# A hybrid decoder layer on one core: weight sums made ahead for ten groups instead of eight, and their casts one step later

## The chip, the cores and the metric

The kernel runs on one core of a Trainium2 chip. A core has five engines that work side by side, each through its own instructions in order: TensorE (PE, matrix products; PEld is its weight load), VectorE (DVE), ScalarE (ACT), GpSimd (POOL) and SyncE (SP, which here issues nearly all transfers). They wait for each other through semaphores. The metric is the time of one execution in microseconds on the device; lower is better.

## What is computed

One decoder layer for 256 tokens of width 2048, all in float32:

```python
h = layer_norm(alpha * h + 0.5 * swiglu(h, w_ffn1_gu, w_ffn1_down))
rq, rk, rv, rg, aq, ak, av, gate_r, gate_a = split(h @ w_in)
ret_branch = (silu(rg) * head_group_norm(retention(rotary(rq), rotary(rk), rv))) @ w_ret_out
att_branch = sliding_window_attention_sinks(rotary(aq), rotary(ak), av) @ w_att_out
mixed = (sigmoid(gate_r) * ret_branch + sigmoid(gate_a) * att_branch) @ w_mix_out
h = layer_norm(alpha * h + mixed)
h = layer_norm(alpha * h + 0.5 * swiglu(h, w_ffn2_gu, w_ffn2_down))
h = layer_norm(alpha * h + sigmoid(h @ w_ple_gate) * (p @ w_ple_proj))
```

The feed-forwards have an inner width of 5632, the retention 8 heads, the attention 16 query heads and 4 key heads with a window of 128.

## The kernel before

**Products of split numbers.** TensorE gets each float32 operand as two parts: a high part, which is the number rounded to the type fp32r (a cast on ScalarE, L98), and a low part, the number less its high part (a subtraction on VectorE, L99). A product is the sum of three: low by high, high by high, high by low (`Sum.add`, L374 to L376). So every 512 KB chunk of weights (128 x 1024 numbers) costs one load on SP, one cast and one subtraction before TensorE can use it. In the features form (`features_chunk`, L325 and L333) the weights are the stationary side.

**Seven products instead of eight.** Two halves of the tokens, two of the inner dimension and two of the outer make a 2 x 2 block product. A unit of kind "P" is one plain pair of chunks: 2 x 12 = 24 matmuls of 512 columns. A unit of kind "S" (`Seven`) gets by with seven products, 21 matmuls, and needs four sums of weights t1 to t4 (VectorE, 128 x 512 each), which are split like weights. A unit of kind "D" (`Prepared`) is the same, but its sums were made and split much earlier and put away in DRAM; the unit loads the four tiles hu, lu, hv, lv (high and low part of u = t1, t3 and of v = t2, t4), one chunk and half of another.

**The second feed-forward** (`ffn("f2", ...)`) has eleven blocks j of columns, each of eight pairs p of the inner dimension. `gu_units` names the kinds: block 0 is plain; blocks with even j have four S; blocks with odd j have three S, or three S and two D (pairs 4 and 5, `AHEAD`) if j stands in `AHEAD_BLOCKS`. The order in a D block is "PPSDSDSP", in the other odd ones "PPSPSPSP". After each block its 128 x 512 result is transposed on TensorE (L906), two chunks into the next block.

**Sums made ahead** (`sums_ahead`) is a generator: each step is one call of `next` from `run_side`, which runs after each chunk or unit of weights, first the next job of the list `side`, then one step of the first generator in the list `lazy`. For each item it makes u (L238, L239), casts it (L240), makes v (L242, L243), casts it (L244), loads the next item's two raw chunks, subtracts (L248 for u, L250 for v) and stores the four tiles (L252, L255); `pause` waits `every` steps between these. Items are listed block by block, pair 4 then pair 5. Items 0 and 1 run during queries and keys of the retention, items 2 to 4 during its values, item 5 during its gates, items 6 and 7 in the last projection of the mixers (`w_mix`).

**Around it.** `fill` loads and splits weights ahead of use as far as a budget of slots and of time allows; `slots_for_weights` sets the budget. All tiles of up to 512 KB share 46 slots. Before unit 0 of a D block the budget is set to `AHEAD_SLOTS - j`. The retention gates (`paired_out(("w_in_f2", grp), ...)`, tiles rg) run with the retention's own work in `side`, two heads at a time: `ret2` (outputs ro on TensorE, L1187, then statistics on VectorE, L1194), `ret2b` (the reciprocal root, ten small instructions, and the normalization, L1206), `ret2c` (times the gate, L1216), `ret3` (four transposes on TensorE, L1225), `ret3b` (L1236, L1237). Each job stands one chunk after the one before; a chunk of gates is twelve matmuls.

The order of the work is written out by hand; nothing is reordered.

Of the kernel before, what the change touches and what calls it, by code (L numbers as in the profile page):

```python
# [39 lines left out]


AHEAD = (4, 5)
AHEAD_BLOCKS = (1, 3, 5, 7)
AHEAD_SLOTS = 32

SEVEN_DOWN = (6, 7, 8, 9)
# [9 lines left out]
def layer(ctx: ExitStack, tc: tile.TileContext, io):  # L56
# [16 lines left out]
    def slot(shape, dt, name):  # L73
        return slots.tile(shape, dt, tag="slot", name=name)
# [144 lines left out]
    def sums_ahead(items, wait, every):  # L219


        def pause():
            for _ in range(every):
                yield

        pairs = [[Chunk(k) for k in items[0]]]
        for _ in range(wait):
            yield
        for j, (key, _) in enumerate(items):
            a, b = pairs.pop()  # L230
            b11, b21, b12, b22 = a.of(a.raw, 0), a.of(a.raw, 1), b.of(b.raw, 0), b.of(b.raw, 1)
            u, v = (slot([P, 2, 512], F32, w + a.name) for w in "uv")
            t1, t3, t2, t4 = (x.rearrange("p (g n) -> p g n", g=2) for x in (u[:, 0], u[:, 1], v[:, 0], v[:, 1]))
            parts = [slot([P, 2, 512], F32R, w + a.name) for w in ("hu", "lu", "hv", "lv")]
            uh, ul, vh, vl = parts
            away = [dram.tile([P, 2, 512], F32, name=f"{w}{a.name}") for w in ("hud", "lud", "hvd", "lvd")]
            put_by_sums[key] = away
            dve.tensor_tensor(t1, b11, b12, ALU.add)  # L238
            dve.tensor_tensor(t3, b12, b22, ALU.add)  # L239
            act.copy(uh, u)  # L240
            yield from pause()
            dve.tensor_tensor(t2, b11, t3, ALU.add)  # L242
            dve.tensor_tensor(t4, t2, b21, ALU.add)  # L243
            act.copy(vh, v)  # L244
            if j + 1 < len(items):
                pairs.append([Chunk(k) for k in items[j + 1]])
            yield from pause()
            dve.tensor_tensor(ul, u, uh, ALU.subtract)  # L248
            yield from pause()
            dve.tensor_tensor(vl, v, vh, ALU.subtract)  # L250
            for e in range(2):
                sync.dma_start(away[e], parts[e].bitcast(F32))  # L252
            yield from pause()
            for e in range(2, 4):
                sync.dma_start(away[e], parts[e].bitcast(F32))  # L255
# [44 lines left out]
    def slots_for_weights(n, ahead=45, far=90):  # L300
        room.update(slots=n, ahead=ahead, far=far)
# [5 lines left out]
    lazy = []  # L307
# [152 lines left out]
    def forms_of(parts, name):  # L460
        hi, lo = (slot([P, 8, P], F32R, name + w) for w in "hl")
        return seven_forms(whole(parts, name + "w"), hi, lo)

    def units_of(order, sevens, ahead=()):

        sevens, ahead = list(sevens), list(ahead)
        plain = [p for p in range(KD // 2) if p not in sevens + ahead]
        of = {"S": sevens, "D": ahead, "P": plain}
        return [(kind, of[kind].pop(0)) for kind in order]
# [382 lines left out]
    def gu_units(name, j):  # L852
        if j == 0:
            return [("P", p) for p in range(KD // 2)]
        if name == "f2" and j in AHEAD_BLOCKS:
            return units_of("PPSDSDSP", SEVEN[:3], AHEAD)
# [3 lines left out]
    def gu_keys(name, j):  # L860
        return lambda n, p: (name + "_gu", j, n, p)
# [26 lines left out]
    def ffn(name, i, ht, norm, keep, residual, keepers, away):  # L888
# [28 lines left out]
        for j in range(KF // 4):  # L917
# [19 lines left out]
            def before(u, j=j, offset=KD // 2 - len(units)):  # L937
# [7 lines left out]
                if j == 0 and u == 7:  # L945
# [3 lines left out]
                    if name == "f2":  # L949
                        g = AHEAD[0] // 2  # L950
                        made[g] = forms_of([ht[:, 4 * g : 4 * g + 4, :]], f"{name}f{g}")
                if name == "f2" and j in AHEAD_BLOCKS and u == 0:
                    slots_for_weights(AHEAD_SLOTS - j)
# [151 lines left out]
    def mixers(ht, norm, residual, keepers, away):  # L1105
# [29 lines left out]
        slots_for_weights(14)  # L1135
        ahead = [(gu_keys("f2", j)(0, p), gu_keys("f2", j)(1, p)) for j in AHEAD_BLOCKS for p in AHEAD]
        lazy.append(sums_ahead(ahead[:2], 3, 2))
        lazy.append(rotary_table("a"))
        lazy.append(sums_ahead(ahead[2:5], 2, 2))
        lazy.append(sums_ahead(ahead[5:6], 3, 4))  # L1140
        for grp in range(8):
            ps = banks(f"rqk{grp}")
            features_out([(("w_in_f", grp), ps)], KD, both_halves)
# [310 lines left out]

        lhs = lambda k: of_pairs(mix_t, k)
        slots_for_weights(16)
        lazy.append(sums_ahead(ahead[6:], 3, 2))
        for blk in range(3):
            if blk == 2:
                load_for_norm(1)  # L1460
# [195 lines left out]
    with tc.manual_schedule():  # L1656
        dve.memset(warm, 0.0)
        for eps, v in roots.items():
            dve.memset(v, 4.0 * eps)
        act.activation(warm, warm, AF.Silu)  # L1660
        plan_ffn("f1")
        plan.extend(Single(("w_pp", blk, 0)) for blk in range(2))
        plan_mixers()
        plan.extend(Single(("w_pp", blk, 0)) for blk in range(2, 4))
        plan_ffn("f2")
        for blk in range(4):
            plan_tokens(("w_pg", blk), KD)
        kept = sorted({p // 2 for p in SEVEN})
        warm_up()
        norm = ffn("f1", 0, ht, None, x_parts, x_columns, (), rows[0])  # L1670
        norm = mixers(norm.new, norm, rows[0], kept, rows[1])
        norm = ffn("f2", 2, norm.new, norm, norm.keep, rows[1], (), None)
        embedding(norm.new, norm, norm.y)
        assert not (plan or loaded or ready or side or lazy) and not room["used"]
# [100 lines left out]
```

## Time and profile before

| | us |
|---|---|
| median of three runs (lowest, highest) | 2276.21 (2275.74, 2276.75) |
| the profiled execution's own time | 2275.9 |
| its span in the profile | 2274.1 |
| TensorE busy | 2262.9 |
| VectorE busy | 1980.2 |
| ScalarE busy | 1219.8 |

The profile is one execution, in which each instruction has a start and a length. Views of it sum instructions by line, tile and operation, list them in order of time, sum them over stretches of the span, or follow the chain of work that ended last back from its end. A tile's name ends in what it holds: hw_in_f is the high part of a chunk of w_in, lw_in_f the low part, rw_in_f the raw chunk. "x4" counts instructions in one row; a figure in brackets is idle time of the engine before the instruction, with what ended it. A matmul's length includes its way through the array: the next one starts before it ends, so distances are taken from start to start. On VectorE too an instruction can start a little before the one ahead of it ends.

### The profile page before, as it was taken

The numbers are of one execution on the slowest core, as the hardware profiler recorded it, in microseconds if no ns is written. First come the engines' busy times: TensorE is split into PE (matmuls) and PEld (weight loads), VectorE is DVE, ScalarE is ACT, GpSimd is POOL, SyncE is SP. The second block draws the span as 40 slices with busy tenths as digits, with TensorE's granted clock in tenths as the row PEclk, the third lists the DMA queues.
The fourth block names the chain that finished last, engine by engine and source line by source line (L and its number), as shares of the span: only waits on it lengthen the run. The fifth ranks groups of instructions, "written<-read, shape, count | busy, mean of one in ns | idle before, by whom it ended". The sixth has DMA issues, their size and how long they took to land.

```text
span 2274.1 us, 29070 instructions
## 1 busy us (share of the span) xinstructions
PE 2262.9 (100%) x10495; PEld 1880.3 (83%) x10495; DVE 1980.2 (87%) x2561; ACT 1219.8 (54%) x1485; POOL 2.2 (0%) x9
## 2 busy tenths in 40 slices
PE   9999999999999999999999999999999999999998
PEld 8888888888888888888778888888888888888886
DVE  7999999999989887787789787789999999889887
ACT  6555555556555444544566454555565556555543
POOL 0000000000000000000000000000000000000000
PEclk9999999999999999999999999999999999999999
DMA  8666665665587789655456567787767766565772
GB/s 300 204 203 196 196 212 177 206 205 190 206 290 255 259 307 310 222 163 169 141 158 221 187 211 268 293 287 237 263 213 260 253 197 216 193 213 189 284 268 75
DMA packets 207592, 505.75 MB, mean 222 GB/s; under 512 B 16076, under 2 KB 19788, under 8 KB 207448
## 3 DMA queue, kind: packets, MB, share of 16 engines
q1 hardware_dynamic: 205320, 501.06, 65.5%
q10 hardware_dynamic: 2128, 2.84, 0.4%
q8 instruction: 82, 1.34, 0.2%
q14 instruction: 62, 0.51, 0.1%
HBM read 478.67 MB, written 25.17 MB: 222 GB/s over the span
## 4 chain that ended last, share of the span: by engine, by line
PE 97%; DVE 1%; DMA 1%; issue 0%; ACT 0%; POOL 0%; DVEq 0%; ACTq 0%; POOLq 0%
PE f1g L376 3%; PE f1g L374 3%; PE f1g L375 3%; PE f2g L376 3%; PE f2g L375 3%; PE f2g L374 3%; PE rqk L325 3%; PE f1u L376 2%; PE f1u L375 2%; PE f1u L374 2%; PE f2u L376 2%; PE f2u L375 2%; PE f2u L374 2%; PE aqk L325 2%; PE f2d L375 2%; PE f1d L375 2%
## 5 line engine op out<-in xcount | busy, mean ns | idle before, releaser
L99 DVE TENSOR_TENSOR lf_gu<-rf_gu,hf_gu 128x1024 fp32r<-128x1024 f32 (+1 forms) x276 | 325.3, 1210 | 14.1 <-ACT hf_gu L98 13.2
L98 ACT CAST hf_gu<-rf_gu 128x1024 fp32r<-128x1024 f32 (+1 forms) x276 | 275.7, 1043 | 31.7 <-DMA rf_gu<-in_f_gu 30.0
L99 DVE TENSOR_TENSOR lf_down<-rf_down,hf_down 128x1024 fp32r<-128x1024 f32 x152 | 181.2, 1219 | 23.6 <-ACT hf_down L98 20.3
L99 DVE TENSOR_TENSOR lw_in_f<-rw_in_f,hw_in_f 128x1024 fp32r<-128x1024 f32 x140 | 167.2, 1218 | 34.5 <-ACT hw_in_f L98 34.5
L98 ACT CAST hf_down<-rf_down 128x1024 fp32r<-128x1024 f32 x152 | 155.6, 1051 | 77.5 <-DMA rf_down<-in_f_down 21.5
L98 ACT CAST huf_gu<-uf_gu 128x1024 fp32r<-128x1024 f32 x70 | 73.7, 1053 | 145.4 <-DVE uf_gu L171 139.7
L98 ACT CAST hw_in_f<-rw_in_f 128x1024 fp32r<-128x1024 f32 x140 | 139.9, 1050 | 1.9 <-PE ga0a L375 1.0
L374 PE MATMUL f1g<-hf_gu,xt 128*128 128x512 f32 x247 | 96.6, 391 | 0.0
L376 PE MATMUL f1g<-lf_gu,xt 128*128 128x512 f32 x247 | 96.4, 390 | 0.0
L375 PE MATMUL f1g<-hf_gu,xt 128*128 128x512 f32 x247 | 96.4, 390 | 0.0
L98 ACT CAST hvf_gu<-vf_gu 128x1024 fp32r<-128x1024 f32 x70 | 73.8, 1054 | 29.5 <-DVE vf_gu L173 28.5
L963 ACT ACTIVATE eve<-eve 128x1024 f32<-128x1024 f32 x20 | 21.2, 1062 | 125.8 <-DVE eve L962 125.8
L374 PE MATMUL f2g<-hf_gu,ht 128*128 128x512 f32 x223 | 87.0, 390 | 0.0
L376 PE MATMUL f2g<-lf_gu,ht 128*128 128x512 f32 x223 | 86.9, 390 | 0.0
L375 PE MATMUL f2g<-hf_gu,ht 128*128 128x512 f32 x223 | 86.8, 389 | 0.0
L99 DVE TENSOR_TENSOR luf_gu<-uf_gu,huf_gu 128x1024 fp32r<-128x1024 f32 x70 | 85.2, 1217 | 0.0
L99 DVE TENSOR_TENSOR lvf_gu<-vf_gu,hvf_gu 128x1024 fp32r<-128x1024 f32 x70 | 85.2, 1217 | 0.0
L374 PE MATMUL f1u<-hf_gu,xt 128*128 128x512 f32 x212 | 83.4, 393 | 0.0
L375 PE MATMUL f1u<-hf_gu,xt 128*128 128x512 f32 x212 | 82.5, 389 | 0.0
L376 PE MATMUL f1u<-lf_gu,xt 128*128 128x512 f32 x212 | 82.5, 389 | 0.0
L374 PE MATMUL f2u<-hf_gu,ht 128*128 128x512 f32 x180 | 71.3, 396 | 0.0
L375 PE MATMUL f2u<-hf_gu,ht 128*128 128x512 f32 x180 | 70.1, 390 | 0.0
(1439 smaller groups left out, 6511.6 us busy)
## 6 DMA issues: line engine op xcount, KB each, us to landing
rf_gu<-in_f_gu SPq DMA_DIRECT2D x358, 512.0 KB
rf_down<-in_f_down SPq DMA_DIRECT2D x176, 512.0 KB
rw_in_f<-in_w_in_f SPq DMA_DIRECT2D x148, 512.0 KB
rw_rv<-in_w_rv SPq DMA_DIRECT2D x32, 512.0 KB
rw_ret<-in_w_ret SPq DMA_DIRECT2D x32, 512.0 KB
rw_mix<-in_w_mix SPq DMA_DIRECT2D x32, 512.0 KB
rw_pg<-in_w_pg SPq DMA_DIRECT2D x32, 512.0 KB
rw_att<-in_w_att SPq DMA_DIRECT2D x16, 512.0 KB
```

Source lines behind the costliest of these rows:

```text
L98: act.copy(dst_hi, src)
L99: (lo_engine or dve).tensor_tensor(dst_lo, src, dst_hi, ALU.subtract)
L325: pe.matmul(ps[f], hi[:, kk, f * P : (f + 1) * P], rhs(k), start=k == 0, stop=k == n_k - 1,)
L374: pe.matmul(o, al, bh, start=first, stop=False)
L375: pe.matmul(o, ah, bh, start=False, stop=False)
L376: pe.matmul(o, ah, bl, start=False, stop=self.left == 0)
L963: act.activation(g, g, AF.Silu)
```

## The change

`AHEAD_BLOCKS` gains block 9, so the list of items grows from eight to ten. The third list of `sums_ahead` takes items 5 to 7 instead of 5 alone, with a first wait of 2 steps instead of 3 and 3 steps between parts instead of 4; items 8 and 9 (block 9) take the place of 6 and 7 in the last projection. Block 9 turns from "PPSPSPSP" to "PPSDSDSP". In `sums_ahead`, the cast of u moves behind the pause, into the step that makes v, and the cast of v moves into the step of the first subtraction, together with the next item's loads.

```diff
-AHEAD_BLOCKS = (1, 3, 5, 7)
+AHEAD_BLOCKS = (1, 3, 5, 7, 9)
...
             dve.tensor_tensor(t1, b11, b12, ALU.add)
             dve.tensor_tensor(t3, b12, b22, ALU.add)
+            yield from pause()
             act.copy(uh, u)
-            yield from pause()
             dve.tensor_tensor(t2, b11, t3, ALU.add)
             dve.tensor_tensor(t4, t2, b21, ALU.add)
+            yield from pause()
             act.copy(vh, v)
             if j + 1 < len(items):
                 pairs.append([Chunk(k) for k in items[j + 1]])
-            yield from pause()
             dve.tensor_tensor(ul, u, uh, ALU.subtract)
             yield from pause()
             dve.tensor_tensor(vl, v, vh, ALU.subtract)
...
-        lazy.append(sums_ahead(ahead[5:6], 3, 4))
+        lazy.append(sums_ahead(ahead[5:8], 2, 3))
...
-        lazy.append(sums_ahead(ahead[6:], 3, 2))
+        lazy.append(sums_ahead(ahead[8:], 3, 2))
```

## The prediction

> **What bounds the kernel now.** The page comes first: busy shares, then the chain of work that ended last.
>
> ```profile
> span 2274.1 us, 29070 instructions
> PE 2262.9 (100%) x10495; PEld 1880.3 (83%) x10495; DVE 1980.2 (87%) x2561; ACT 1219.8 (54%) x1485; POOL 2.2 (0%) x9
> PE 97%; DVE 1%; DMA 1%; issue 0%; ACT 0%; POOL 0%; DVEq 0%; ACTq 0%; POOLq 0%
> ```
>
> TensorE is idle for 2274.1 - 2262.9 = 11.2 us, and 97% of the chain is its own. A busy PE need not be a fast one, so I asked next for stretches: queries and keys of the retention, retention gates, then blocks 1 and 9 of the second feed-forward (columns: PE, weight load, DVE, ACT, POOL; clock; DMA share; GB/s).
>
> ```profile
> 733.80:823.20 89.40, 89.40 (x513) 78.69 (x513) 78.02 (x116) 40.34 (x55) 0.00 (x0) 1.00 0.79 275
> 888.50:1000.00 111.50, 111.18 (x570) 94.43 (x569) 87.72 (x196) 52.59 (x69) 0.00 (x0) 1.00 0.70 222
> 1531.50:1572.50 41.00, 41.00 (x188) 34.05 (x187) 36.19 (x44) 22.16 (x26) 0.00 (x0) 1.00 0.70 229
> 1862.40:1904.80 42.40, 42.40 (x193) 35.22 (x192) 38.22 (x44) 23.44 (x27) 0.00 (x0) 1.00 0.59 183
> ```
>
> PE idles only in the retention gates (0.32 us), at full clock everywhere. So a shorter VectorE or ScalarE brings nothing by itself; what counts is the number of matmuls, and whether added work makes PE wait where it now just doesn't. The chain dates the blocks by the transposes that follow each (start, us):
>
> ```profile
> 1531.52 0.87 PE f2t L906 x8
> 1572.54 0.87 PE f2t L906 x8
> ...
> 1862.40 0.87 PE f2t L906 x8
> 1904.78 0.87 PE f2t L906 x8
> ```
>
> Block 1 (three S and two D groups of seven products) takes 1572.54 - 1531.52 = 41.02 us, block 9 (three S, the rest plain) 1904.78 - 1862.40 = 42.38.
>
> **Block 9 gets two D groups.** By its units it becomes a copy of block 1, two groups of 21 matmuls instead of 24. Both blocks' windows show PE without a gap, so the difference is the gain: 42.38 - 41.02 = 1.36 us, 0.227 us for each of six matmuls. The Trainium skill ("TensorE: Matmul & The Clock Gate", Back-to-back issue gap) gives about 131 ns between matmuls of 512 columns in a sustained stream; by it the six would save 0.79 us. The trace has 227 ns, so the sum stays with the blocks. The eight added loads of sums and their share of DMA (0.70 in block 1 against 0.59) are in block 1's window already.
>
> **Casts one step behind.** Now uh and vh are cast in the step that makes u and v, so ScalarE, which works in order, waits for VectorE with weight casts behind it. The groups between 700 and 1450 us (busy, mean ns | idle before, releaser):
>
> ```profile
> L99 DVE TENSOR_TENSOR lw_in_f<-rw_in_f,hw_in_f 128x1024 fp32r<-128x1024 f32 x140 | 167.2, 1218 | 34.5 <-ACT hw_in_f L98 34.5
> L98 ACT CAST hw_in_f<-rw_in_f 128x1024 fp32r<-128x1024 f32 x140 | 139.9, 1050 | 1.9 <-PE ga0a L375 1.0 <-PE rg L375 0.3 <-PE ga0b L375 0.3
> L240 ACT CAST huf_gu<-uf_gu 128x1024 fp32r<-128x1024 f32 x8 | 8.4, 1050 | 41.7 <-DVE uf_gu L239 41.7
> L244 ACT CAST hvf_gu<-vf_gu 128x1024 fp32r<-128x1024 f32 x8 | 8.4, 1050 | 28.6 <-DVE vf_gu L243 25.7 <-PE rv L376 2.8
> L248 DVE TENSOR_TENSOR luf_gu<-uf_gu,huf_gu 128x1024 fp32r<-128x1024 f32 x8 | 9.7, 1218 | 0.0
> ```
>
> The 41.7 + 25.7 us of ScalarE's waits, and most of VectorE's 34.5 us behind them, should go. I cost this at 0: where they occur PE has no gap (733.80 to 823.20). The cover is weights that are split before PE needs them; it grows. The next pair's raw loads leave one step later and queue behind the same weight loads on SP. No sum and no w_in_f cast now waits for DMA in these rows, so 0 too; a loss would be one load's lateness, and behind a late sum on VectorE stand the subtractions for the next weights. The stores keep their step after the last subtraction; the third list's steps come every three chunks instead of four, which spends the same work sooner.
>
> **Two more groups between 930 and 1010 us.** Items 5 to 7 run in one list, the last two during the retention gates and after them. Each adds four sums of 0.68 us and two subtractions of 1.22 on VectorE, two casts of 1.05 on ScalarE, two raw loads and four stores of 512 KB on SP. ScalarE (52.59 of 111.50 us busy) and DMA (0.70) have room. VectorE is 79% busy, but its order matters: PE's transposes of head h (L1225) wait for the product at L1216, the last of a long chain on VectorE. In the timelines, PE first, then VectorE:
>
> ```profile
> 947.81 0.39 PE L376 MATMUL rg<-lw_in_f,ht 128*128 128x512 f32 x1
> 948.42 0.66 PE L1225 MATMUL rt<-ident,ron 128*128 128x128 f32 x4 [0.22 <-DVE ron L1216]
> 977.25 0.39 PE L376 MATMUL rg<-lw_in_f,ht 128*128 128x512 f32 x1
> 977.74 0.66 PE L1225 MATMUL rt<-ident,ron 128*128 128x128 f32 x4
> 1007.41 0.60 PE L1225 MATMUL rt<-ident,ron 128*128 128x128 f32 x4
> ```
> ```profile
> 910.41 0.68 DVE L238 TENSOR_TENSOR uf_gu<-rf_gu,rf_gu 128x512 f32<-128x512 f32 x1
> 911.02 0.68 DVE L239 TENSOR_TENSOR uf_gu<-rf_gu 128x512 f32<-128x512 f32 x1
> 933.63 1.22 DVE L248 TENSOR_TENSOR luf_gu<-uf_gu,huf_gu 128x1024 fp32r<-128x1024 f32 x1
> 934.76 1.22 DVE L99 TENSOR_TENSOR lw_in_f<-rw_in_f,hw_in_f 128x1024 fp32r<-128x1024 f32 x1
> 936.37 0.42 DVE L1194 BATCH_NORM_STATS2 gst<-ro 128x6 f32<-128x256 f32 x1
> 947.68 0.68 DVE L1216 TENSOR_TENSOR ron<-ron,rgs 128x512 f32<-128x512 f32 x1
> 965.67 0.43 DVE L1194 BATCH_NORM_STATS2 gst<-ro 128x6 f32<-128x256 f32 x1 [1.60 <-PE ro L1187]
> 977.00 0.69 DVE L1216 TENSOR_TENSOR ron<-ron,rgs 128x512 f32<-128x512 f32 x1
> 1006.42 0.68 DVE L1216 TENSOR_TENSOR ron<-ron,rgs 128x512 f32<-128x512 f32 x1
> ```
> ```profile
> 935.12 1.07 PE ro L1187 x9
> ...
> 964.56 1.09 PE ro L1187 x9
> ```
>
> A matmul follows its forerunner by 0.227 us, so PE waits at head 2 for 948.42 - 947.81 - 0.227 = 0.38 us and at head 4 for 0.26; the product ends 0.06 us before its transposes (948.36, 948.42). At head 6 it ends at 1007.10 for a start at 1007.41: 0.25 us to spare. Each chain starts when PE ends a head's output (965.67, 1.11 us after the start at 964.56), so work put ahead of that start goes into the wait of 1.60 us, and work put behind it delays the transposes in full. The changed order puts behind it: at head 2 the two sums of the first added group (L238, L239; 911.02 - 910.41 = 0.61 each, 1.22), at head 4 one subtraction (L250; as 934.76 - 933.63 = 1.13), at head 6 another (L248, 1.13). At head 2 the chain now starts at 936.37 and could at 935.12 + 1.11 = 936.23, 0.14 earlier, with the late casts gone. So PE waits longer by 1.22 - 0.14 = 1.08, by 1.13, and by 1.13 - 0.25 = 0.88: 3.09 us. Low end: 0, and -0.64 if the present waits go as well. High end: 3 x (1.22 + 1.13) = 7.1, if a sum and a subtraction fell behind each start; the order doesn't show that.
>
> In the mixing stage two groups keep their place, with other keys: 0.
>
> **The slots of blocks 9 and 10.** The budget falls from 25 to 23 before block 9 and stays there in block 10. At the third S of block 7 VectorE waited for raw loads behind the eight loads of sums; in block 10 the fourth S is ready just ahead of PE:
>
> ```profile
> 1790.28 0.68 DVE L99 TENSOR_TENSOR bf_gu<-rf_gu_5b,bf_gu 128x512 fp32r<-128x512 f32 x1
> 1794.46 0.69 DVE L170 TENSOR_TENSOR uf_gu<-rf_gu,rf_gu 128x512 f32<-128x512 f32 x1 [3.50 <-DMA rf_gu<-in_f_gu]
> ...
> 1927.64 1.22 DVE L99 TENSOR_TENSOR lvf_gu<-vf_gu,hvf_gu 128x1024 fp32r<-128x1024 f32 x1
> ```
> ```profile
> 1929.76 0.39 PE L376 MATMUL f210s<-lvf_gu,f2fh 128*128 128x512 f32 x1
> ```
>
> Block 9 will repeat the 3.50 us. Block 10 has 1929.76 - 1928.86 - 0.06 = 0.84 us to spare. If nothing of the delay carries over, 0; if all, 3.50 - 0.84 = 2.66. Block 7's wait cost PE nothing, nor did block 8 after it, so I take a value near zero, 0.4.
>
> **Sum.** -1.36 + 3.09 + 0.4 = +2.1 us. The profiled execution has a span of 2274.1 and a time of 2275.9, 1.8 around it; this becomes 2276.2 and 2278.0. It lies 0.3 below the median of the runs, 2276.21, so on that scale 2278.3.
>
> **Rivals.** (a) The transposes don't wait longer, because the earlier part of the chain shrinks: -1.36, or with the 0.64 gone -2.0: 2274.2 to 2274.9. For it: VectorE's 34.5 us of waits for casts vanish. Against it: head 4's chain starts at PE, not at a cast. (b) The DMA wait of block 9 reaches block 10 whole: -1.36 + 3.09 + 2.66 = +4.4, 2280.6, and over +4.55 if the wait exceeds 3.50 us as slots get fewer. For it: one more block's results hold slots; against it: block 8. (c) Slower: VectorE is the true bound. It takes over as soon as its backlog outlasts the split weights in store; then all that it is given counts: 2 x (4 x 0.68 + 2 x 1.22) = 10.3, less in block 9, where two full subtractions per group become one and a half:
>
> ```profile
> L99 DVE TENSOR_TENSOR lf_gu<-rf_gu,hf_gu 128x1024 fp32r<-128x1024 f32 x123 | 145.6, 1217 | 0.3 <-ACT hf_gu L98 0.3
> L99 DVE TENSOR_TENSOR bf_gu<-rf_gu,bf_gu 128x512 fp32r<-128x512 f32 x35 | 23.9, 684 | 0.0
> ```
>
> 2 x (1.217 - 0.684) = 1.07 less, so 10.3 - 1.07 = +9.2; fewer matmuls then bring nothing: 2285.4. For it: 87% busy; against it: PE has no gaps where VectorE has 88% (78.02 of 89.40). The Trainium skill ("Perfetto Trace Analysis", Identifying the Most-Contended Engine) judges TensorE by its weight loads, not its matmuls, and names the engine of highest occupancy: here VectorE's 87% over 83%. By that rule (c) would hold; the windows without a PE gap speak against it. (d) The change does what it says and more: ScalarE's freed 67 us show up in the time. PE's idle time in these stages (0.32 us) leaves nothing to collect; over 0.2% faster would need waits that the trace hides.
>
> **Chances.** A measurement of this kernel tells about 0.2% (4.55 us) from no change. Forecast 0.50 (+0.5 to +4, a small tail of 0.03 slower than 0.2%); (a) 0.20; (b) 0.16, of it 0.12 over the bound; (c) 0.08; (d) 0.06, of it 0.05 faster. So faster 0.05, slower 0.03 + 0.12 + 0.08 = 0.23, within 0.72. The range runs from (a) to a little above (b): 2274.2 to 2282.0, leaving out (c) and most of (d).
>
> **What would show it.** Right: block 9 at 41.02 us between transposes; ScalarE's idle before L240 and L244 near zero; PE gaps before the transposes of heads 2, 4 and 6 of 1.5, 1.4 and 0.9 us; no gap in queries and keys. Wrong: those gaps unchanged (then a); a gap in block 10 over 1 us behind a longer wait at L170 (b); PE gaps spread over the gate stage before weight matmuls (c).

## The result and the profile after

| | before | after |
|---|---|---|
| median of 17 runs each on one chip, us (lowest, highest) | 2276.10 (2275.31, 2277.20) | 2280.43 (2279.55, 2281.05) |
| ratio, 95% interval | | 1.0019 [1.0012, 1.0025] |
| span of the profiled execution, us | 2274.1 | 2278.7 |

The changed kernel is 4.3 us slower, 0.19%: small, but the interval of the ratio lies above 1, and every run of it lies above every run of the kernel before. From here on a kernel is read by its distance to the runs of the kernel before on its own chip, since these medians lie between 2275.7 and 2276.1.

Span, busy shares and chain on the page of the kernel after:

```profile
span 2278.7 us, 29120 instructions
PE 2263.0 (99%) x10489; PEld 1877.9 (82%) x10489; DVE 1989.2 (87%) x2573; ACT 1224.6 (54%) x1489; POOL 2.2 (0%) x9
PE 94%; DVE 3%; DMA 1%; issue 1%; ACT 1%; DVEq 0%; ACTq 0%
```

VectorE has 9 us more to do, but its share is the same 87%. What changed is the chain: VectorE now holds 3% of it instead of 1%. So the question is where TensorE waits. The view of TensorE's waits (what it waited for: us in all, times, longest), kernel after:

```profile
PE rt L1225 <- DVE ron L1216: 3.4, 3, 1.3
...
PE f210s L374 <- ACT f2a L908: 1.0, 1, 1.0
...
PE f29s L376 <- DVE lvf_gu L99: 0.2, 1, 0.2
```

Two places: three transposes of the retention's heads, and block 9 with block 10 behind it. The timeline of TensorE at the heads:

```profile
949.52 0.66 PE L1225 MATMUL rt<-ident,ron 128*128 128x128 f32 x4 [1.31 <-DVE ron L1216]
...
978.35 0.39 PE L376 MATMUL rg<-lw_in_f,ht 128*128 128x512 f32 x1
979.98 0.66 PE L1225 MATMUL rt<-ident,ron 128*128 128x128 f32 x4 [1.24 <-DVE ron L1216]
...
1010.69 0.63 PE L1225 MATMUL rt<-ident,ron 128*128 128x128 f32 x4 [0.86 <-DVE ron L1216]
```

By the prediction's measure (start to start, less 0.227) head 4 waits 979.98 - 978.35 - 0.227 = 1.40 us and head 2 in the same way 1.47. Ahead of head 6 stand eight matmuls of 256 columns, which start at 1008.72 and without a wait take 0.95 us (1006.46 to 1007.41 in the kernel before), so it waits 1010.69 - 1008.72 - 0.95 = 1.02. The timeline of VectorE at head 4 shows why, in the order that the prediction read out of the program:

```profile
976.06 1.00 DVE L1206 TENSOR_SCALAR ron<-ro,gmv,grs 128x256 f32<-128x256 f32 x2
976.97 1.22 DVE L250 TENSOR_TENSOR lvf_gu<-vf_gu,hvf_gu 128x1024 fp32r<-128x1024 f32 x1
978.10 1.22 DVE L99 TENSOR_TENSOR lw_in_f<-rw_in_f,hw_in_f 128x1024 fp32r<-128x1024 f32 x1
979.24 0.69 DVE L1216 TENSOR_TENSOR ron<-ron,rgs 128x512 f32<-128x512 f32 x1
```

The added subtraction (L250) stands between the head's normalization and its product with the gate, and TensorE starts when the product ends.

The transposes that bound blocks 9 and 10 (start, us), first in the kernel after, then, from its chain, those that end block 10 in the kernel before (the prediction shows the ones at 1904.78); and the casts and subtractions of the sums with what their engines waited for (kernel after, groups, 700 to 1450 us):

```profile
1865.82 1.04 PE L906 MATMUL f2t<-ident,evw 128*128 128x128 f32 x8
1907.44 1.04 PE L906 MATMUL f2t<-ident,evw 128*128 128x128 f32 x8
...
1950.93 1.04 PE L906 MATMUL f2t<-ident,evw 128*128 128x128 f32 x8
```
```profile
1946.48 0.87 PE f2t L906 x8
```
```profile
L99 DVE TENSOR_TENSOR lw_in_f<-rw_in_f,hw_in_f 128x1024 fp32r<-128x1024 f32 x140 | 167.3, 1219 | 22.5 <-ACT hw_in_f L98 22.2 <-issue 0.2
...
L241 ACT CAST huf_gu<-uf_gu 128x1024 fp32r<-128x1024 f32 x10 | 10.5, 1054 | 17.3 <-DVE uf_gu L239 16.5 <-PE rv L375 0.9
L245 ACT CAST hvf_gu<-vf_gu 128x1024 fp32r<-128x1024 f32 x10 | 10.5, 1050 | 6.5 <-DVE vf_gu L243 5.8 <-PE rv L376 0.7
```

Block 9 takes 41.62 us instead of 42.38, not 41.02: it has gaps of its own. Block 10 takes 1950.93 - 1907.44 = 43.49 us, where it took 1946.48 - 1904.78 = 41.70. ScalarE's waits before the casts fell from 41.7 + 25.7 to 16.5 + 5.8 us; ten groups wait less than eight did.

Last, block 9's third group that VectorE sums itself. VectorE and ScalarE there, in their timelines, and TensorE where it stalls in block 10:

```profile
1883.87 0.69 DVE L170 TENSOR_TENSOR uf_gu<-rf_gu,rf_gu 128x512 f32<-128x512 f32 x1 [6.15 <-PE f2g L376]
```
```profile
1882.49 1.05 ACT L98 CAST hf_gu<-rf_gu 128x1024 fp32r<-128x1024 f32 x1 [7.15 <-DMA rf_gu<-in_f_gu]
1883.85 0.62 ACT L98 CAST bf_gu<-rf_gu 128x512 fp32r<-128x512 f32 x1 [0.30 <-DMA rf_gu<-in_f_gu]
...
1911.90 1.05 ACT L98 CAST huf_gu<-uf_gu 128x1024 fp32r<-128x1024 f32 x1 [2.67 <-DVE uf_gu L171]
1913.35 1.05 ACT L98 CAST hvf_gu<-vf_gu 128x1024 fp32r<-128x1024 f32 x1 [0.40 <-DVE vf_gu L173]
1914.30 1.07 ACT L908 COPY f2a<-f2t 128x512 f32<-128x512 f32 x2
```
```profile
1913.54 0.39 PE L376 MATMUL f210s<-luf_gu,f2fh 128*128 128x512 f32 x1
1914.93 0.50 PE L374 MATMUL f210s<-huf_gu,f2fl 128*128 128x512 f32 x1 [1.01 <-ACT f2a L908]
1915.27 0.40 PE L375 MATMUL f210s<-huf_gu,f2fh 128*128 128x512 f32 x1
```

VectorE waits 6.15 us at L170. The row names a matmul that ended at about that moment, but ScalarE waits for the same raw weights at the same time and names the DMA (7.15 and 0.30, the second cast starting at 1883.85, beside VectorE's 1883.87): the wait is for the load. From there the lateness runs on. TensorE loses 0.33 us at the third group's last sums (1890.75). In block 10 the S groups come late on VectorE, so the cast hv waits for them (1913.35), and the copies of block 9's transposes (L908) stand behind that cast in ScalarE's queue; they free the buffer of results (a PSUM bank) that TensorE writes to next: 1914.93 - 1913.54 - 0.227 = 1.16 us. At 1934.20 another 0.31, before the matmul of the fourth S group that the prediction watched; its subtraction lvf ends at 1934.15. The three gaps make 1.8 us. The blocks lose more: 41.62 - 41.02 = 0.60 and 43.49 - 41.70 = 1.79, together 2.4. More than half of the difference is in the matmuls right behind a gap, which follow by 0.34 us (1915.27 - 1914.93) instead of 0.227.

### The profile page after: what moved, and what is told of

Read it like the earlier page. It is cut to its first block, busy times and chain, and to the rows that moved or that the text cites. A ratio compares the mean times of both kernels' runs of the same rounds, so it can differ in the third digit from the quotient of the medians.

```text
span 2278.7 us, 29120 instructions
## 1 busy us (share of the span) xinstructions
PE 2263.0 (99%) x10489; PEld 1877.9 (82%) x10489; DVE 1989.2 (87%) x2573; ACT 1224.6 (54%) x1489; POOL 2.2 (0%) x9
## 4 chain that ended last, share of the span: by engine, by line
PE 94%; DVE 3%; DMA 1%; issue 1%; ACT 1%; DVEq 0%; ACTq 0%
PE f1g L376 3%; PE f1g L374 3%; PE f1g L375 3%; PE rqk L325 3%; PE f1u L375 2%; PE f1u L376 2%; PE f1u L374 2%; PE f2g L374 2%; PE f2g L375 2%; PE f2g L376 2%; PE f2u L374 2%; PE f2u L376 2%; PE f2u L375 2%; PE f1d L374 2%; PE f2d L375 2%; PE aqk L325 2%
## 5 line engine op out<-in xcount | busy, mean ns | idle before, releaser
L99 DVE TENSOR_TENSOR lw_in_f<-rw_in_f,hw_in_f 128x1024 fp32r<-128x1024 f32 x140 | 167.3, 1219 | 22.5 <-ACT hw_in_f L98 22.2
L374 PE MATMUL f2g<-hf_gu,ht 128*128 128x512 f32 x217 | 84.6, 390 | 0.0
L375 PE MATMUL f2g<-hf_gu,ht 128*128 128x512 f32 x217 | 84.4, 389 | 0.0
L374 PE MATMUL f2u<-hf_gu,ht 128*128 128x512 f32 x172 | 68.2, 397 | 0.0
L376 PE MATMUL f2u<-lf_gu,ht 128*128 128x512 f32 x172 | 67.0, 389 | 0.0
```

Of the source, the lines that this page charges most:

```text
L99: (lo_engine or dve).tensor_tensor(dst_lo, src, dst_hi, ALU.subtract)
L374: pe.matmul(o, al, bh, start=first, stop=False)
L375: pe.matmul(o, ah, bh, start=False, stop=False)
L376: pe.matmul(o, ah, bl, start=False, stop=self.left == 0)
```

## The experiments

All compare with the kernel after; "over before" is the difference of medians to the runs of before on the same chip. The diffs are against the changed kernel, but for the first.

### The reordered casts alone

The kernel before with only the new order in `sums_ahead`; eight groups and their lists stay.

```diff
+            yield from pause()
             act.copy(uh, u)
-            yield from pause()
             dve.tensor_tensor(t2, b11, t3, ALU.add)
             dve.tensor_tensor(t4, t2, b21, ALU.add)
+            yield from pause()
             act.copy(vh, v)
...
-            yield from pause()
```

> The kernel before with the reordered casts alone: eight groups, the old four lists. My theory (the casts' waits lie beside a PE that has no gap): the time of before, 2276.1, within 0.7 us; ScalarE's idle time before the casts at L240/L244 (41.7 + 25.7 us before) falls to near zero; PE's waits before the transposes at L1225 stay within 0.3 us of before's. Rival (the freed 67 us of ScalarE show in the time): at least 2 us faster than before, 2274 or less.

Measured 2276.18 against 2276.0, ratio 1.0 [0.9991, 1.0008]: no change. The casts (now L241 and L245) still wait, but far less:

```profile
L241 ACT CAST huf_gu<-uf_gu 128x1024 fp32r<-128x1024 f32 x8 | 8.4, 1055 | 8.5 <-DVE uf_gu L239 7.7 <-PE rv L375 0.9
L245 ACT CAST hvf_gu<-vf_gu 128x1024 fp32r<-128x1024 f32 x8 | 8.4, 1053 | 6.6 <-DVE vf_gu L243 5.8 <-PE rv L376 0.7
```

These groups of this kernel (700 to 1450 us) have 7.7 + 5.8 us where the kernel before had 41.7 + 25.7. TensorE's waits before heads 2 and 4 are 0.27 and 0.26 us (0.38 and 0.26 before). Some 54 us of freed ScalarE time are worth nothing by themselves; rival (d) falls.

### Three groups in the gates, eight in all

```diff
-AHEAD_BLOCKS = (1, 3, 5, 7, 9)
+AHEAD_BLOCKS = (1, 3, 5, 7)
...
-        lazy.append(sums_ahead(ahead[8:], 3, 2))
```

> The changed kernel with eight groups instead of ten: block 9 is as before, and all eight are made by the end of the gates, three of them in the list of the gates; none in the mixing stage. VectorE gets as much work as in the kernel before, in other places. My theory (sums behind the start of a head's chain delay PE's transposes one for one): PE waits before L1225 of heads 2, 4 and 6 are 1.5, 1.4 and 1.0 us as in the changed kernel, no gap in blocks 9 and 10, 2276.1 + 3.2 = 2279.3. Rival (the amount of VectorE's work decides): 2276.1, as before.

Measured 2279.07, 3.1 over before, ratio 1.0015 [1.0006, 1.0024]. VectorE does the same sums as in the kernel before and the time still rises by 3.1. The view of TensorE's waits has those of the kernel after at the heads and none of f29s or f210s, blocks 9 and 10:

```profile
PE rt L1225 <- DVE ron L1216: 3.4, 3, 1.3
```

So the place of the sums costs, not their amount; rival (c) falls here.

### No step of the sums between a head's output and its transposes

The list `held` is filled when a head's output is issued and emptied at its transposes; while it holds something, `run_side` takes no step of the sums.

```diff
-    side = []
+    side, held = [], []
...
-        if lazy and next(lazy[0], "end") == "end":
+        if lazy and not held and next(lazy[0], "end") == "end":
...
-                s = keep.pop(("s", h))
+                s, held[:] = keep.pop(("s", h)), [h]
...
-                for e in range(2):
+                for e in held.clear() or range(2):
```

> The changed kernel with ten groups, but no step of the sums is taken between a head's output (L1187) and its transposes (L1225): the steps are taken in the chunks that are left, and the list ends later. My theory: the three long PE waits before L1225 go, and what the kernel before had there (0.38 and 0.26 us) with them; blocks 9 and 10 keep their gaps; 2280.4 - 3.2 - 0.6 = 2276.6. Rival (the amount of VectorE's work decides, or the waits move to the later chunks): 2280.4, with PE gaps spread over the gates or just after them.

Measured 2276.49, 0.5 over before, ratio 1.0002 [0.9993, 1.001], where the kernel after is 4.3 over: 3.8 us less, with all ten groups made. The three waits are gone from the view of TensorE's waits; 0.27 and 0.26 us at heads 2 and 4 stay (start to start), so those have another cause than the sums, and the expectation was wrong in that part. Block 10 keeps its wait in that view:

```profile
PE f210s L374 <- ACT f2a L908: 1.0, 1, 1.0
```

### Block 9's units in another order

```diff
-            return units_of("PPSDSDSP", SEVEN[:3], AHEAD)
+            return units_of("PPSDSDSP" if j < 9 else "PPDSDSSP", SEVEN[:3], AHEAD)
```

> The changed kernel with the units of block 9 in another order: P P D S D S S P instead of P P S D S D S P, so that the last sums ahead are loaded earlier and no loads of sums come between those of the second and the third group that VectorE sums itself. My theory (the third such group of block 9 gets its raw weights and slots too late, because the loads of sums take their places ahead of it; block 10 starts late by that, and the copies of block 9's result on ScalarE stand behind its casts): PE's gaps of 0.34, 1.17 and 0.31 us at 1890, 1914 and 1934 shrink to under 0.5 in all, 2280.4 - 1.5 = 2278.9. Rival (two D groups and one more block's result are too many slots in any order): 2280.4, gaps of the same sum.

Measured 2278.44, 2.4 over before, ratio 1.001 [1.0001, 1.0019]: 1.9 us less than the kernel after. The waits at the heads stay. Block 9 has no gap left (41.01 us between its transposes); in block 10 the wait for f2a is gone from the view, and start to start 0.22 us are left at the same matmul and 0.28 later, 0.5 in all. So two D groups in block 9 are not too many as such; the order in which their loads leave counts.

### Ten groups with the old order of casts

```diff
-            yield from pause()
             act.copy(uh, u)
+            yield from pause()
...
-            yield from pause()
             act.copy(vh, v)
...
+            yield from pause()
```

> The changed kernel with ten groups, but with the casts again in the step of their sums, as in the kernel before. The prediction's term (the reorder costs and brings 0): 2280.4 within 0.7 us. Rival (with eight groups the casts' waits were hidden, with three groups in the gates they are not: ScalarE stands behind VectorE's sums with the weight casts behind it, and VectorE's subtractions wait for those): at least 2 us slower, 2282.5 or more, with PE waits in the gates that are longer than 1.5, 1.4 and 1.0 us, or before weight matmuls.

Measured 2294.07, 18.1 over before, ratio 1.008 [1.0067, 1.0094]: without the reorder ten groups would cost another 13.8 us. The view of TensorE's waits, and the groups of the casts and of VectorE's subtractions:

```profile
PE rt L1225 <- DVE ron L1216: 11.2, 4, 3.5
```
```profile
L99 DVE TENSOR_TENSOR lw_in_f<-rw_in_f,hw_in_f 128x1024 fp32r<-128x1024 f32 x140 | 167.3, 1220 | 40.4 <-ACT hw_in_f L98 40.4
...
L240 ACT CAST huf_gu<-uf_gu 128x1024 fp32r<-128x1024 f32 x10 | 10.5, 1050 | 50.5 <-DVE uf_gu L239 50.5
```

11.2 - 3.4 = 7.8 us of it are waits at the heads. Most of the rest has a cause that the waits view doesn't show: the clock. Stretches of this kernel (start and end, length, busy time of TensorE, clock, DMA share, GB/s):

```profile
918.70:922.20 3.50, 0.34 (x2) 0.98 0.67 248
922.20:924.60 2.40, 2.34 (x8) 0.50 0.05 15
```

After 3.2 us of idle time the granted clock is 0.50 for a while, and matmuls follow each other by 0.427 us instead of 0.227. The Trainium skill ("TensorE: Matmul & The Clock Gate", Part 1: The HAM clock gate) says that the array falls to half its clock after about one idle window of 3.4 us; the row is close to that, a little below it (the last section has a much shorter wait). Three of the four waits are followed by such a stretch, idle times of 3.22, 3.46 and 3.23 us; the matmuls behind them take 1.5, 1.5 and 2.6 us longer than the same ones in the kernel after, 5.6 in all. 7.8 + 5.6 = 13.4 of the 13.8.

### The old order of casts with the steps held back

The steps held back as above, 28 slots as in the next experiment, and the casts as in the one above; a single run.

> The kernel of the run before this one (steps held back, 28 slots), with the casts again in the step of their sums. Theory one (the old order of casts hurt ten groups only where steps stood in a head's chain): the same time as with the new order, 2273.8 to 2275. Theory two (it also makes ScalarE and VectorE late behind one another in the gates whatever the steps): PE waits of several us between 950 and 1050, 2278 or more.

Measured 2280.53, 4.8 over before; the same kernel with the new order of casts is 1.4 under (last experiment), so the order is worth some 6.3 us here, as far as a single run tells. The view of TensorE's waits shows them back at the heads, though no step stands in a head's chain, and in the attention:

```profile
PE rt L1225 <- DVE ron L1216: 2.8, 2, 2.1
PE at L1343 <- DVE asc L1333: 1.9, 2, 1.6
```

Theory two is right: the time is over 2278, and ScalarE and VectorE are late behind one another. At head 6 the timelines of ScalarE and VectorE show the chain of waits:

```profile
993.61 1.05 ACT L240 CAST huf_gu<-uf_gu 128x1024 fp32r<-128x1024 f32 x1 [4.09 <-DVE uf_gu L239]
```
```profile
996.61 1.23 DVE L99 TENSOR_TENSOR lw_in_f<-rw_in_f,hw_in_f 128x1024 fp32r<-128x1024 f32 x1 [3.03 <-ACT hw_in_f L98]
```

ScalarE waits for the sum u, its next weight cast starts only at 995.53, and VectorE waits for that cast; the statistics that begin head 6's chain stand behind it on VectorE (998.22).

### More slots for block 9

```diff
-                    slots_for_weights(AHEAD_SLOTS - j)
+                    slots_for_weights(AHEAD_SLOTS - j if j < 9 else 28)
```

> The changed kernel with a budget of 28 slots from block 9 on instead of 23. The prediction put the cost of blocks 9 and 10 on this budget. My theory (with more room the second loads of sums leave one unit earlier, and the raw weights of the third group that VectorE sums, which queue behind them, are there in time): PE's gaps at 1890, 1914 and 1934 shrink from 1.8 to 0.5 us or less in all, 2280.4 - 1.5 = 2278.9, as with the other order of units. Rival (the slots are in fact taken by results, so a larger budget only moves the wait from the program's order to the slots): 2280.4 and the same gaps.

Measured 2277.76, 1.8 over before, ratio 1.0008 [0.9998, 1.0017]: 2.5 us less than the kernel after, and no gap is left in blocks 9 and 10. SyncE's timeline shows what moved, first the kernel after, then this one (raw weights, then the second D group's half chunk, 5b, which leaves with its four tiles of sums):

```profile
1855.12 14.63 SPq L112 DMA_DIRECT2D rf_gu<-in_f_gu  x3
1869.85 0.97 SPq L201 DMA_DIRECT2D rf_gu_5b<-in_f_gu  x1
```
```profile
1855.05 3.39 SPq L112 DMA_DIRECT2D rf_gu<-in_f_gu  x3
1858.53 0.42 SPq L201 DMA_DIRECT2D rf_gu_5b<-in_f_gu  x1
```

The loads leave 11.3 us earlier. The raw weights of the third group leave when they did (1872.72, and 1872.85 in the kernel after), but the loads of sums no longer run just ahead of them, and VectorE's wait at L170 shrinks from 6.15 us (timeline of VectorE, this kernel):

```profile
1878.29 0.69 DVE L170 TENSOR_TENSOR uf_gu<-rf_gu,rf_gu 128x512 f32<-128x512 f32 x1 [0.73 <-DMA rf_gu<-in_f_gu]
```

### Block 7's budget for block 9

```diff
-                    slots_for_weights(AHEAD_SLOTS - j)
+                    slots_for_weights(AHEAD_SLOTS - min(j, 7))
```

> The changed kernel with a budget of 25 slots from block 9 on, the value that blocks 7 and 8 have, instead of 23. The prediction's step (it is the fall from 25 to 23 that makes blocks 9 and 10 dearer): the gaps of blocks 9 and 10, 1.8 us in all, fall to near zero. My theory (with 25 the second loads of sums still leave no earlier, since they need three more than are left; what differs from block 7 is how many slots are really free): the same gaps, 1.5 to 2 us, and 2280.4 within 0.8.

A single run: 2280.96, 5.3 over before, with the gaps of the kernel after (0.33, 1.15 and 0.32 us) and VectorE's wait in the timeline as long as there:

```profile
1883.84 0.69 DVE L170 TENSOR_TENSOR uf_gu<-rf_gu,rf_gu 128x512 f32<-128x512 f32 x1 [6.29 <-PE f2g L376]
```

The two slots between block 7's budget and block 9's are not the cause. What counts is whether the budget admits the second D group before the block's first S group is done, in the order of the program: by the accounts that `fill` keeps, 28 does, 25 and 23 don't.

### One subtraction made twice

In the third list L250 is made twice (same values).

```diff
-    def sums_ahead(items, wait, every):
+    def sums_ahead(items, wait, every, twice=False):
...
-            dve.tensor_tensor(vl, v, vh, ALU.subtract)
+            for _ in range(1 + twice): dve.tensor_tensor(vl, v, vh, ALU.subtract)
...
-        lazy.append(sums_ahead(ahead[5:8], 2, 3))
+        lazy.append(sums_ahead(ahead[5:8], 2, 3, True))
```

> The changed kernel with the subtraction at L250 made twice for the three groups of the third list (the same values twice; 1.13 us more of VectorE each). My theory (only work behind the start of a head's chain counts, and that one for one): the copy for item 6 stands behind the start of head 4: PE's wait there grows from 1.40 by 1.13 to 2.5 us; the copy for item 5 stands ahead of head 2's start, where VectorE has 0.46 us of idle time to take it, so 1.47 + 0.67 = 2.1; head 6 keeps 1.0; in all 2280.4 + 1.8 = 2282.2. Rival (VectorE's work counts as such): three times 1.13, 2283.8; other rival (VectorE catches up): 2280.4.

Measured 2283.66, ratio 1.0035 [1.0021, 1.0049]: 7.7 over before, so 3.4 us more than the kernel after, where I had expected 1.8 and the rival 3.4. By the time alone the rival would have won; the trace decides otherwise. The waits (start to start, less 0.227) are 2.17, 2.66 and 1.02 us: head 2 grew by 0.70 (expected 0.67), head 4 by 1.26 (1.13), head 6 not at all. That is 1.96. The rest stands behind head 2, in TensorE's timeline and in the stretches of this kernel (columns as above):

```profile
949.67 0.66 PE L1225 MATMUL rt<-ident,ron 128*128 128x128 f32 x4 [2.02 <-DVE ron L1216]
950.09 0.53 PE L374 MATMUL rg<-hw_in_f,ht 128*128 128x512 f32 x1
950.41 0.63 PE L375 MATMUL rg<-hw_in_f,ht 128*128 128x512 f32 x1
950.84 0.63 PE L376 MATMUL rg<-lw_in_f,ht 128*128 128x512 f32 x1
```
```profile
950.40:953.80 3.40, 3.40 (x9) 0.50 0.07 11
953.80:960.00 6.20, 6.20 (x31) 1.00 0.68 207
```

For 3.4 us the clock is 0.50; eight matmuls take 0.2 us more each, 1.6 in all. 1.96 + 1.6 = 3.6, against 3.4 in the medians.

### Both costs taken out

First the steps held back with block 9's other order of units, then the steps held back with 28 slots (the edits as above).

> The changed kernel with the steps held back between a head's output and its transposes, and with the units of block 9 in the order P P D S D S S P: the two edits together. My theory (the two costs are independent): 2280.4 - 3.9 - 2.0 = 2274.5, of which 1.36 less than before is block 9's six matmuls; the only PE gap that the kernel before doesn't have is 0.3 us in block 10. Rival (the list that now ends later, or the earlier loads, make a new wait): 2276 or more.

> The changed kernel with the steps of the sums held back between a head's output and its transposes, and a budget of 28 slots from block 9 on. My theory (the two costs are independent, and nothing of either is left): 2280.4 - 3.9 - 2.7 = 2273.8, 2.2 us under the kernel before, of which 1.36 are block 9's six matmuls; no PE gap that the kernel before doesn't have. Rival (what is gained in one place is lost in another): 2274.7 or more, as with the other order of units.

Measured 2274.67 against 2275.97, ratio 0.9995 [0.9986, 1.0004], and 2274.26 against 2275.7, ratio 0.9993 [0.9984, 1.0002]. Each edit takes out its own cost beside the other, and neither kernel has a gap left in blocks 9 and 10. The first came out as expected, but for the 0.3 us in block 10, which aren't there. The second is 1.4 us under before, where I had expected 2.2 from the medians; 1.4 is about what block 9's six matmuls are worth. All its 11 runs (2273.89 to 2274.49) lie under all 15 runs of before (2274.97 to 2277.09), though the interval of the ratio still holds 1. Block 9 is now what the prediction took it for, 1902.80 - 1861.79 = 41.01 us, in TensorE's timeline:

```profile
1861.79 1.04 PE L906 MATMUL f2t<-ident,evw 128*128 128x128 f32 x8
1902.80 1.04 PE L906 MATMUL f2t<-ident,evw 128*128 128x128 f32 x8
```

## Why the prediction was right, and where it was not

**Block 9's six matmuls, -1.36.** Right: 42.38 - 41.01 = 1.37 where nothing delays the block. The 0.227 us per matmul of the trace held.

**The casts, 0.** Right for the kernel before (0.2 us, within the noise), but not an edit with no value: in a kernel with ten groups it is worth 13.8 us, or some 6.3 (a single run) with the sums out of the heads' chains. The prediction costed each edit against the kernel before and did not ask what the other edits would cost without this one. Its sign "near zero" for ScalarE's idle time before these casts didn't come: it was too generous with the waits. ScalarE's fell by two thirds (to 16.5 + 5.8 us), VectorE's 34.5 us by a third (to 22.5), without consequence. Queries and keys stayed without a gap, as forecast (TensorE is busy in all of 733.80 to 823.20).

**The heads, 3.09.** Right, and in each place: 1.09, 1.14 and 1.02 us of added wait against 1.08, 1.13 and 0.88, 3.25 in all; 3.1 measured with that part alone. What made it right was to look at the order on VectorE from the point where TensorE starts the chain: of some 2 x 5.2 us of added VectorE work the path saw three pieces. Rival (a) had the earlier part of the chain shrink; beyond the 0.14 us at head 2 that the sum had counted, it didn't.

**Blocks 9 and 10, 0.4.** This is the step that failed, a size and its reason. It measured 2.4 us, 1.8 of it in three gaps, and block 9 took 41.62 us where 41.02 was to be the sign of right. I took a value near zero because block 7's wait of 3.50 us had cost TensorE nothing, and assumed that "Block 9 will repeat the 3.50 us". It waited 6.15, and the named cause, the budget's fall from 25 to 23, changes nothing. In this term rival (b) was right and the forecast wrong: (b) described the path (block 9's wait for loads reaching block 10) and priced its own part at up to 2.66, and its sign, a gap in block 10 over 1 us behind a longer wait at L170, is there with 1.16 us behind 6.15. Only 0.31 us came by the S group that I had watched (0.84 us to spare); the larger part came by way of ScalarE, whose copies of the transposes stood behind casts that waited, and neither the sum nor (b) had that. Why block 9's second loads leave later than block 7's was not tried. By the program each block's transposed result keeps one of the 46 slots, so block 9 has two fewer than block 7; that this is the reason is likely, but not shown.

**The sum.** -1.36 + 3.25 + 2.39 = +4.3, and 4.3 were measured. The parts fit the experiments: gates alone 3.25 (3.1 measured), without blocks 9 and 10 -1.36 + 3.25 = 1.9 (1.8), without either -1.36 (-1.4). With the steps held back alone the two blocks lose 0.18 + 1.79 = 1.97 by their transposes, so -1.36 + 1.97 = 0.6 (0.5). The forecast itself, +2.1, was half of what came. The range held the time because its upper end went by rival (b), +4.4, not because the sum was near.

## What to carry to other kernels

Work added to an engine that is not the bound cost, in this kernel, what stood between the event that starts a chain and the last result that the bounding engine waits for, one for one as long as the clock held, and nothing elsewhere; so read the order from that event, and put optional work ahead of it. A transfer that is late without cost in one block is not free in the next: ask what room is left there, and follow the lateness through the queues of all engines, also into copies that only free a buffer. An edit worth nothing by itself may be what makes another affordable, so cost the edits together as well as one by one.

## What was not expected of the hardware

A wait of TensorE can cost more than its length. After 2.02 us of idle time the granted clock was 0.50 for 3.4 us (950.4 to 953.8), which added 1.6 us; but after 2.50 us at head 4 of the same execution it stayed at 1.00:

```profile
980.00:983.00 3.00, 0.49 (x4) 1.00 0.34 135
983.00:990.00 7.00, 7.00 (x35) 1.00 0.82 257
```

The Trainium skill ("TensorE: Matmul & The Clock Gate", Part 1: The HAM clock gate) describes a free-running window of about 3.4 us; a stretch of 3.4 us at half clock agrees with it. But the Trainium skill asks there for about one idle window, and a wait of 2.02 us, well below it, was enough here; the measurement decides. With a free-running window it could matter where a wait falls as well as how long it is, which would fit the two rows; no run here tests that. The waits of the kernel after, up to 1.3 us, did not bring it about: its granted clock is 1.00 around them, so its three waits added up one for one.
